# Background sums redistributed over a decoder trunk's stages, and the first feed-forward's SiLUs issued behind the following weight split

## The chip, the cores and the metric

The kernel runs on one core of a Trainium2 chip. The metric is the device time of one execution in microseconds (us); the time before is the median of three runs, 1927.47 us (1927.08 to 1927.84). Everything here is about one program of about 12,000 instructions on five engines: PE (matrix products), ACT (activation functions and copies), DVE (elementwise work and sums), POOL (small odd work) and SP (issues the weights' DMA transfers). PEld in the profile is the loading of the stationary operand of a matrix product.

## The reference

Two layers over 256 tokens of width 2048. Layer 0 mixes by causal pooling, layer 1 by latent attention; each is followed by a SwiGLU feed-forward network (FFN) of width 5632. Each sub-layer's norm is shifted and scaled, and its residual gated, by vectors made from one conditioning vector `c`.

```python
sc = silu(c)
for i in range(2):
    shift_m, scale_m, gate_m, shift_f, scale_f, gate_f = split(sc @ mod_w[i] + mod_b[i], 6)
    if i == 1:
        kv_shift, kv_scale = split(sc @ kv_mod_w + kv_mod_b, 2)
        h_kv = rmsnorm(x, kv_in_norm) * (1 + kv_scale) + kv_shift
        ckv = rmsnorm(h_kv @ w_dkv, kv_norm)
        k_nope, v, k_rope = ckv @ w_uk, ckv @ w_uv, rope(h_kv @ w_kr)
    h = rmsnorm(x, norm_mix[i]) * (1 + scale_m) + shift_m
    if i == 0:
        y = pool_mixer(h)
    else:
        cq = rmsnorm(h @ w_dq, q_norm)
        y = attention(rope(cq @ w_uq), k_nope, k_rope, v) @ w_o
    x = x + gate_m * y
    h = rmsnorm(x, norm_ffn[i]) * (1 + scale_f) + shift_f
    x = x + gate_f * ((silu(h @ w_gate) * (h @ w_up)) @ w_down)
return rmsnorm(x, final_norm)
```

## The kernel before

**Weight units.** Weights arrive as units of 512 x 512 numbers (one 1 MB transfer into a `raw` tile, six of which rotate). Each unit is split into two halves of higher and lower bits: the upper half is a copy on ACT (line 374, tile `hl`), the lower a subtraction on DVE (line 376, another `hl`). Six `hl` tiles rotate, so three units can be ahead of PE. A product of a unit with 256 tokens is 24 matmuls of 128x512 (line 398: upper weights with both halves of the activations, then lower weights) or, for keys and queries, which come out transposed, 48 of 128x256 (line 1296). Two tokens' blocks ("tok") go to two PSUM banks (`ps`); in the last unit of a sum the first bank's twelve matmuls stand ahead of the second's, so that it can be read earlier.

**Background sums.** The products of `silu(c)` with the modulation weights that are not needed at once are made on DVE: `Part.unit` loads 128 rows of the transposed weights (1 MB, a `raw` tile too, line 210) and multiplies and sums them along the row in one instruction (line 211). 168 such sums stand in a list. `split` calls `tick` before each weight unit; `tick` adds a rate to a credit and issues a sum for each whole credit, until a goal (a number left in the list) is met. `plan(left, units)` and `release(left, units)` set the goal and the rate = (sums left in the list - goal)/units. From `hold` (near the end of an FFN) to `release` no sum is issued. After the sixteenth sum of a gate, DVE adds the bias (line 300) and `spread` turns the column on PE (line 292) and sends it through DRAM to all partitions.

**Stages.** In the order of time: the pooling layer; the first FFN (eleven chunks of 512, in the steps of `FFN_STEPS`: p projects a chunk to gate and up, t turns the chunk for the down product, d is a down product of a group); a handover whose order is written by hand (`then_attention`); keys and values in four groups, each one `w_uk` unit (line 1296) and one `w_uv` unit (line 398); between them the modulated input of the queries (`hidden_q`: transposes on PE, line 540, then lines 558 and 559 on ACT and 560 on DVE), then four `w_dq` units for the queries' latent, whose norm is lines 1246 to 1249 (ACT squares and sums, DVE, a power on POOL at line 1248, DVE scales) and which is turned (line 540) and split (lines 1259 on ACT, 1261 on DVE); the heads' weights `w_uq` (split on lines 1458 and 1459; first product on line 1370); attention by head pairs; the output product; the second FFN.

**What sets the order.** Outside the stretches written by hand, a scheduler of the recording layer sets each engine's order when the program is built, by priorities and its own estimate of when operands are there; `issue_after` makes it put an instruction behind a named one. Each engine then works strictly in that order, and waits at the first instruction whose operand isn't there. Functions put into `pending` are called in `flush` at the next split and issued behind that split's two instructions. SiLUs of a chunk (line 802) are in the program right behind the gate's last product; each reads one bank. Then come the up product's units, and DVE multiplies both (line 806); the result is turned on PE (line 729) and split (lines 732 and 733).

**The numbers.** When the first FFN is planned, 144 sums are left, of which 48 belong to the second FFN. With `MIX_LATE` 14, 82 are spread over 93 units; 92 units tick before `hold`, which makes 81 sums. `release` then finds 63 and goes down to 48 + `MIX_DQ` = 54: 9 sums over `MLA_UNITS` = 4 units (2, 2, 2 and 3). The `w_uv` unit of the third group has none. `plan(n_all, DQ_UNITS)` gives the last 6 to the next units at 1.2 each; as the program is built, one stands beside each of the six units that follow (four `w_dq`, `w_uk` and `w_uv` of the fourth group).

Of the kernel before, what the change touches and what calls it, by code (L numbers as in the profile page):

```python
# [13 lines left out]
AF = mybir.ActivationFunctionType  # L14
# [46 lines left out]
BEGUN = 6  # L61
ASIDE = 5

FFN0_UNITS, MLA_UNITS, DQ_UNITS, WO_UNITS, FFN1_UNITS = 93, 4, 5, 8, 60

KNOWN = (1, 3, 5, 7, 9, 10, 11, 12)


LATE, MIX_LATE, MIX_DQ = 3, 14, 6

V_C, V_NM, V_NF, V_KVIN, V_KVN, V_QN, V_PS, V_B, V_KB, V_END = 0, 16, 48, 80, 96, 100, 104, 120, 312, 344

# [21 lines left out]
def tile_trunk(ctx: ExitStack, tc: tile.TileContext, a: dict, out: bass.AP):  # L94
    nc = tc.nc
    sync, act, dve, pe, pool = nc.sync, nc.scalar, nc.vector, nc.tensor, nc.gpsimd
# [20 lines left out]
    def t2k(shape, dt=F32):  # L117
        return work.tile(shape, dt, tag="t2k", bufs=7, name=nm("t2k"))
# [152 lines left out]
    pending = []  # L271
# [307 lines left out]
    def stream_aside(l):  # L579
        if l == 0:  # L580
            return
        aside[l] = dram.tile([P, NT, D], F32, name=nm("aside"))
        with tc.issue_after(w_load[0].ins):
            sync.dma_start(aside[l], x)
# [129 lines left out]
    def ffn(l, hT, gate_name, begun, then):  # L714
# [3 lines left out]
        def project(c, which):  # L718
            if c in begun:
                begun[c][which].block(ND - 1, hT[ND - 1])  # L720
                return begun[c][which].result()
            return proj(ffn_weights(l)[which][:, c], hT)
# [67 lines left out]
        def project_chunk(c):  # L790
            if c == ASIDE:
                stream_aside(l)
            if c == NF - 1:
                end = StreamEnd(l)
                stream_end.append(end)
                for n, wait in enumerate(KNOWN):
                    pending.append((wait, lambda n=n: end.known(n // NT, n % NT, gates[gate_name])))
            gb = project(c, GATE)
            nat[c] = []
            for tok in range(NT):  # L800
                sg = t2k([P, CH])
                act.activation(sg, gb[tok], AF.Silu)  # L802
                nat[c].append(sg)
            ub = project(c, UP)
            for tok in range(NT):
                dve.tensor_tensor(out=nat[c][tok], in0=ub[tok], in1=nat[c][tok], op=ALU.mult)  # L806

        for step in FFN_STEPS:
            {"p": project_chunk, "t": transposed, "d": down}[step[0]](int(step[1:]))
# [848 lines left out]
```

## Time and profile before

| | |
|---|---|
| median of three runs | 1927.47 us (1927.08 to 1927.84) |
| the profiled execution | 1927.86 us, of which the span from first to last instruction is 1926.1 us |
| mean granted TensorE clock | 0.987 of full speed |
| ACT busy | 830.0 us (43%) |
| bytes read from HBM | 567.76 MB, 298 GB/s over the span |
| PE busy in 950 to 985 us (keys and values) | 29.28 of 35.00 us |

The page of the profile gives busy time for each engine, then the span in 40 slices, then the chain of work that ended last, followed back from the end. A busy engine is not a bound by itself; what bounds is read from the waits of the engine that is on the chain, and from what released them. A row of the timeline has the start in us, the length, the engine, line and operation, what is written and read, the shape, how many equal instructions were put together, and in brackets the engine's idle time before it and who ended it.

### The profile page before, as it was taken

How to read it: one execution, taken by the hardware profiler on the slowest of the kernel's cores; microseconds unless marked ns; L12 is line 12 of the kernel's file. 1: busy time of each engine (PE TensorE's matmuls, PEld its weight loads, DVE VectorE, ACT ScalarE, POOL GpSimd, SP SyncE). 2: the span in 40 equal slices, each digit the busy share in tenths (PEclk: the TensorE clock that was granted, in tenths of full speed). 3: DMA queues.
4: the chain of work that ended last, by engine and by line, in shares of the span. 5: the costliest groups of instructions: out<-in, count | busy, mean ns of one | idle time of the engine just before them, and what ended most of it. 6: DMA issues, size and time to landing. Idle time of an engine off the chain costs nothing.

```text
span 1926.1 us, 21857 instructions
## 1 busy us (share of the span) xinstructions
PE 1863.2 (97%) x8797; PEld 1508.1 (78%) x8797; DVE 1412.7 (73%) x1394; ACT 830.0 (43%) x904; POOL 20.9 (1%) x30
## 2 busy tenths in 40 slices
PE   7689999999999999999989999999999999999998
PEld 3256888888888888887879888888888888888887
DVE  2148799999788778789897886889786566645566
ACT  3125643443433334344665745634444433433343
POOL 0000000000000000000100000000000000000000
PEclk9889999999999999999999999999999999999999
DMA  9999998889989899896595394988776666665551
GB/s 398 393 418 417 370 358 340 320 312 357 364 346 380 328 353 353 351 379 260 210 379 199 123 363 180 399 333 319 268 286 240 233 243 245 243 225 209 218 197 44
DMA packets 81655, 575.51 MB, mean 299 GB/s; under 512 B 8929, under 2 KB 9361, under 8 KB 13201
## 3 DMA queue, kind: packets, MB, share of 16 engines
q1 hardware_dynamic: 81026, 570.94, 77.1%
q0 software_dynamic: 432, 3.15, 0.4%
q8 instruction: 69, 1.13, 0.2%
q14 instruction: 32, 0.26, 0.0%
q10 hardware_dynamic: 96, 0.02, 0.0%
HBM read 567.76 MB, written 6.32 MB: 298 GB/s over the span
## 4 chain that ended last, share of the span: by engine, by line
PE 90%; DMA 4%; DVE 3%; ACT 1%; issue 1%; SPq 0%; POOL 0%; POOLq 0%; DVEq 0%; ACTq 0%
PE ps L398 75%; DMA raw<-in_mod_w_dram 3%; PE ps L256 2%; PE ps L1296 2%; PE ps L977 2%; PE ps L407 2%; DVE hl L376 1%; PE ps L729 1%; DVE raw L211 1%; PE ps L1475 1%; ACT hl L374 1%; PE ps L1208 1%; DMA raw<-in_mod_block_dram 0%; DMA raw<-in_w_uk_dram 0%; PE ps L196 0%
## 5 line engine op out<-in xcount | busy, mean ns | idle before, releaser
L398 PE MATMUL ps<-hl,act 128*128 128x512 f32 x6672 | 1526.9, 390 | 8.6 <-ACT hl L374 6.5
L398 PEld LDWEIGHTS ps<-hl,act 128*128 128x128 f32 x6672 | 1251.7, 188 | 272.1 <-ACT hl L374 8.4
L376 DVE TENSOR_TENSOR hl<-raw,hl 128x2048 fp32r<-128x2048 f32 x286 | 653.8, 2289 | 247.9 <-ACT hl L374 247.3
L374 ACT ACTIVATE hl<-raw 128x2048 fp32r<-128x2048 f32 x286 | 546.6, 1918 | 604.1 <-PE ps L398 433.8
L211 DVE SCALAR_TENSOR_TENSOR raw<-raw,s_row 128x2048 f32<-128x2048 f32 x168 | 383.0, 2285 | 2.0 <-DMA raw<-in_mod_wt_dram 2.0
L256 PE MATMUL ps<-raw,s_strip 128*32 128x512 f32 x392 | 63.2, 739 | 36.5 <-DMA raw<-in_mod_w_dram 36.2
L698 DVE TENSOR_TENSOR act<-ps,act 128x512 f32<-128x512 f32 x96 | 64.5, 685 | 17.2 <-PE ps L398 17.2
L256 PEld LDWEIGHTS ps<-raw,s_strip 128*32 128x32 f32 x392 | 9.4, 119 | 69.3 <-DMA raw<-in_mod_w_dram 45.9
L1296 PE MATMUL ps<-act,hl 128*128 128x256 f32 x384 | 49.5, 286 | 1.1 <-DVE hl L376 1.1
L1296 PEld LDWEIGHTS ps<-act,hl 128*128 128x128 f32 x384 | 48.1, 194 | 1.8 <-DVE hl L376 1.3
L407 PE MATMUL ps<-hl,act 128*128 128x512 f32 x192 | 47.0, 398 | 1.1 <-DVE hl L520 0.9
L802 ACT ACTIVATE t2k<-ps 128x512 f32<-128x512 f32 x24 | 14.2, 590 | 71.7 <-PE ps L398 71.7
L407 PEld LDWEIGHTS ps<-hl,act 128*128 128x128 f32 x192 | 35.2, 188 | 10.6 <-ACT act L490 1.5
L742 DVE TENSOR_TENSOR x<-ps,x 128x512 f32<-128x512 f32 x32 | 21.8, 689 | 28.8 <-PE ps L398 28.8
L732 ACT ACTIVATE act<-ps 128x512 fp32r<-128x512 f32 x44 | 23.3, 594 | 43.2 <-PE ps L729 30.5
L263 DVE COPY t2k<-ps 128x256 f32<-128x256 f32 x4 | 1.7, 425 | 52.8 <-ACT t2k L262 52.8
L427 ACT ACTIVATE junk<-x 128x512 bf16<-128x512 f32 x23 | 14.5, 630 | 54.5 <-DVE x L612 37.3
L806 DVE TENSOR_TENSOR t2k<-ps,t2k 128x512 f32<-128x512 f32 x24 | 16.6, 690 | 28.7 <-PE ps L398 28.7
L520 DVE TENSOR_TENSOR hl<-raw,hl 128x2048 fp32r<-128x2048 f32 (+2 forms) x16 | 31.8, 1987 | 5.7 <-ACT hl L517 5.7
L977 PEld LDWEIGHTS ps<-act,act 128*128 128x128 f32 x128 | 25.0, 202 | 11.7 <-issue 8.4
L977 PE MATMUL ps<-act,act 128*128 128x256 f32 x128 | 32.4, 406 | 0.0
L696 ACT ACTIVATE act<-ps 128x512 f32<-128x512 f32 x32 | 19.1, 597 | 28.7 <-PE ps L398 28.6
(221 smaller groups left out, 927.4 us busy)
## 6 DMA issues: line engine op xcount, KB each, us to landing
raw<-in_mod_wt_dram SPq DMA_DIRECT2D x136, 1024.0 KB, 6.7
raw<-in_ffn_gate_dram SPq DMA_DIRECT2D x88, 1024.0 KB, 6.3
raw<-in_ffn_up_dram SPq DMA_DIRECT2D x88, 1024.0 KB, 5.9
raw<-in_ffn_down_dram SPq DMA_DIRECT2D x88, 1024.0 KB, 4.9
raw<-in_mod_w_dram SPq DMA_DIRECT2D x48, 1024.0 KB, 11.7
raw<-in_kv_mod_wt_dram SPq DMA_DIRECT2D x32, 1024.0 KB, 7.6
raw<-in_w_o_dram SPq DMA_DIRECT2D x16, 1024.0 KB, 7.2
raw<-in_mod_block_dram SPq DMA_DIRECT2D x8, 1024.0 KB, 12.4
```

The lines of the kernel that those rows point to most:

```text
L211: dve.scalar_tensor_tensor(out=r, in0=r, scalar=1.0, in1=s_row, op0=ALU.mult, op1=ALU.mult, accum_out=self.sums[:, self.n:self.n + 1])
L256: pe.matmul(self.bank[m * STRIP:(m + 1) * STRIP, :], lhsT=weights(k), rhs=r[:, k, i, :], start=first, stop=last)
L374: hi_ins = act.activation(hi, r, AF.Copy)
L376: lo_ins = dve.tensor_tensor(out=lo, in0=r, in1=hi.bitcast(F32), op=ALU.subtract)
L398: pe.matmul(banks[tok], lhsT=t_[:, i, k, tok * P:(tok + 1) * P], rhs=w[:, k, :], start=first and n < len(part), stop=last and n >= len(ord ...
L407: pe.matmul(bank, lhsT=t_[:, i, k, tok * P:(tok + 1) * P], rhs=w[:, k, :], start=first and n == 0, stop=last and n == len(order) - 1)
L520: dve.tensor_tensor(out=w[2][:, ks], in0=w[0][:, ks], in1=w[1][:, ks].bitcast(F32), op=ALU.subtract)
L698: dve.tensor_tensor(out=part, in0=banks[tok], in1=part, op=ALU.add)
L732: act.activation(m[:, 0, :, ts_], v, AF.Copy)
L742: dve.tensor_tensor(out=sums, in0=bank, in1=sums, op=ALU.add)
L977: pe.matmul(mixed[g][:, n % 2, :], lhsT=wp[g][:, k, ns], rhs=pool_all[g // 2][:, g % 2, k, :], start=k == 0, stop=k == KL - 1)
L1296: pe.matmul(pt[:, h, :], lhsT=w(h0 + h, k), rhs=t_[:, i, k, :], start=n == 0, stop=n == 3 * KL - 1)
```

## The change

Three numbers change, and one line of `ffn`.

```diff
--- before.py
+++ after.py
@@ -61,12 +61,12 @@
 BEGUN = 6
 ASIDE = 5
 
-FFN0_UNITS, MLA_UNITS, DQ_UNITS, WO_UNITS, FFN1_UNITS = 93, 4, 5, 8, 60
+FFN0_UNITS, MLA_UNITS, DQ_UNITS, WO_UNITS, FFN1_UNITS = 93, 4, 6, 8, 60
 
 KNOWN = (1, 3, 5, 7, 9, 10, 11, 12)
 
 
-LATE, MIX_LATE, MIX_DQ = 3, 14, 6
+LATE, MIX_LATE, MIX_DQ = 3, 12, 7
 
 V_C, V_NM, V_NF, V_KVIN, V_KVN, V_QN, V_PS, V_B, V_KB, V_END = 0, 16, 48, 80, 96, 100, 104, 120, 312, 344
 
@@ -799,7 +799,7 @@
             nat[c] = []
             for tok in range(NT):
                 sg = t2k([P, CH])
-                act.activation(sg, gb[tok], AF.Silu)
+                pending.append((0, lambda sg=sg, bank=gb[tok]: act.activation(sg, bank, AF.Silu)))
                 nat[c].append(sg)
             ub = project(c, UP)
             for tok in range(NT):
```

`MIX_LATE` 12 instead of 14 leaves two sums fewer for after the first FFN: 84 over 93 units, 83 by `hold`. `release` finds 61 and goes down to 48 + 7 = 55: 6 sums over four units (1, 2, 1 and 2). `plan(n_all, DQ_UNITS)` spreads the last 7 over 6 units, 7/6 each (five units with one, the last with two). From the first key unit to the heads there are 13 sums instead of 15. The SiLUs go into `pending` with no wait, and so are issued behind both instructions of the next split, which is that of the first unit of the up product. All 22 SiLU pairs of both FFNs go this way.

The built programs have the same instructions on each engine; their order differs. The first place is ACT in the first FFN, seventh to eighth projected chunk; `hl` of line 374 is the upper half of a weight unit, `t2k` of line 802 the SiLU's result, `ps` its bank. Before:

```order
L374 ACTIVATE hl_4029<-raw_4024 128x2048
L374 ACTIVATE hl_4062<-raw_4057 128x2048
L802 ACTIVATE t2k_4090<-ps_3954 128x512
L374 ACTIVATE hl_4101<-raw_4096 128x2048
L802 ACTIVATE t2k_4092<-ps_3955 128x512
L374 ACTIVATE hl_4134<-raw_4129 128x2048
```

Now:

```order
L374 ACTIVATE hl_4032<-raw_4027 128x2048
L374 ACTIVATE hl_4065<-raw_4060 128x2048
L374 ACTIVATE hl_4102<-raw_4097 128x2048
L802 ACTIVATE t2k_4093<-ps_3957 128x512
L802 ACTIVATE t2k_4094<-ps_3958 128x512
L374 ACTIVATE hl_4137<-raw_4132 128x2048
```

The split that stood between the two SiLUs stands ahead of both. The same happens in the three other chunks of the first FFN that had this order; the chunks that had both SiLUs behind the split keep it, and on PE's side the second FFN's waits are on the same instructions as before.

The second place is ACT in the third key group. `hl_6518<-raw_6516` before and `hl_6515<-raw_6513` now are the split of the same `w_uv` unit, the one that follows the transposes of the queries' input on PE; lines 558 and 559 modulate that input; lines 1288 and 1297 copy finished values and keys out of PSUM. Before:

```order
L1288 ACTIVATE act_6310<-ps_6376 128x512
L1297 ACTIVATE act_6415<-ps_6431 128x512
L1297 ACTIVATE act_6415<-ps_6457 128x512
L558 ACTIVATE t2k_6498<-ps_6483,cols 128x256
L558 ACTIVATE t2k_6502<-ps_6483,cols 128x256
L559 ACTIVATE act_6497<-t2k_6498 128x256
L559 ACTIVATE act_6497<-t2k_6502 128x256
L558 ACTIVATE t2k_6506<-ps_6488,cols 128x256
L558 ACTIVATE t2k_6510<-ps_6488,cols 128x256
L559 ACTIVATE act_6497<-t2k_6506 128x256
L559 ACTIVATE act_6497<-t2k_6510 128x256
L374 ACTIVATE hl_6518<-raw_6516 128x2048
```

Now:

```order
L1288 ACTIVATE act_6313<-ps_6378 128x512
L374 ACTIVATE hl_6515<-raw_6513 128x2048
L1288 ACTIVATE act_6313<-ps_6379 128x512
L1297 ACTIVATE act_6415<-ps_6428 128x512
L374 ACTIVATE hl_6601<-raw_6596 128x2048
L1297 ACTIVATE act_6415<-ps_6454 128x512
L558 ACTIVATE t2k_6495<-ps_6480,cols 128x256
```

The `w_uv` split, and that of the first `w_dq` unit (`hl_6601`), stood behind the eight modulations and stand ahead of them now, the first of them two copies earlier still.

The third place is where the queries' latent is normed and the attention's gate is finished, on DVE and PE. `raw` on line 211 is a sum, lines 1247 and 1249 the norm of the two token blocks, line 376 here the lower half of the fourth group's `w_uv` unit, line 300 the gate's bias. DVE before:

```order
L1247 TENSOR_SCALAR sm_6750<-sm_6749 128x1
L211 SCALAR_TENSOR_TENSOR raw_6769,sums_5661<-raw_6769,s_row 128x2048
L1249 TENSOR_SCALAR t2k_6752<-ps_6580,sm_6751 128x512
L1247 TENSOR_SCALAR sm_6759<-sm_6758 128x1
L1249 TENSOR_SCALAR t2k_6761<-ps_6581,sm_6760 128x512
L376 TENSOR_TENSOR hl_6856<-raw_6849,hl_6855 128x2048
L211 SCALAR_TENSOR_TENSOR raw_6851,sums_5661<-raw_6851,s_row 128x2048
L1261 SCALAR_TENSOR_TENSOR act_6838<-ps_6828,vcol,act_6838 128x256 x2
L1459 TENSOR_TENSOR hl_6890<-raw_6887,hl_6889 128x1536
L1261 SCALAR_TENSOR_TENSOR act_6838<-ps_6833,vcol,act_6838 128x256 x2
L1459 TENSOR_TENSOR hl_6948<-raw_6945,hl_6947 128x1536
L300 TENSOR_TENSOR cols<-sums_5661,vcol 128x16
```

DVE now:

```order
L211 SCALAR_TENSOR_TENSOR raw_6766,sums_5587<-raw_6766,s_row 128x2048
L1247 TENSOR_SCALAR sm_6747<-sm_6746 128x1
L1249 TENSOR_SCALAR t2k_6749<-ps_6577,sm_6748 128x512
L376 TENSOR_TENSOR hl_6856<-raw_6846,hl_6855 128x2048
L1247 TENSOR_SCALAR sm_6756<-sm_6755 128x1
L211 SCALAR_TENSOR_TENSOR raw_6848,sums_5587<-raw_6848,s_row 128x2048
L1249 TENSOR_SCALAR t2k_6758<-ps_6578,sm_6757 128x512
L211 SCALAR_TENSOR_TENSOR raw_6851,sums_5587<-raw_6851,s_row 128x2048
L1261 SCALAR_TENSOR_TENSOR act_6835<-ps_6825,vcol,act_6835 128x256 x2
L300 TENSOR_TENSOR cols<-sums_5587,vcol 128x16
L1459 TENSOR_TENSOR hl_6890<-raw_6887,hl_6889 128x1536
```

One sum stands ahead of the first norm and one between the two halves of the second; the subtraction of the `w_uv` unit, which stood behind both norms, stands between them; line 300 stands ahead of both subtractions of line 1459 instead of behind the two. On PE, the transposes of the normed latent (line 540) before:

```order
L1296 MATMUL ps_6802<-act_6199,hl_6772 128x256 x4
L540 MATMUL ps_6828<-con,t2k_6752 128x128
L540 MATMUL ps_6828<-con,t2k_6761 128x128
L540 MATMUL ps_6828<-con,t2k_6752 128x128
L540 MATMUL ps_6828<-con,t2k_6761 128x128
L540 MATMUL ps_6833<-con,t2k_6752 128x128
L540 MATMUL ps_6833<-con,t2k_6761 128x128
L540 MATMUL ps_6833<-con,t2k_6752 128x128
L540 MATMUL ps_6833<-con,t2k_6761 128x128
L398 MATMUL ps_6847<-hl_6855,act_6199 128x512 x8
```

Now:

```order
L1296 MATMUL ps_6799<-act_6205,hl_6769 128x256 x4
L540 MATMUL ps_6825<-con,t2k_6749 128x128
L540 MATMUL ps_6830<-con,t2k_6749 128x128
L398 MATMUL ps_6844<-hl_6855,act_6205 128x512 x5
L540 MATMUL ps_6825<-con,t2k_6758 128x128
L540 MATMUL ps_6825<-con,t2k_6749 128x128
L540 MATMUL ps_6825<-con,t2k_6758 128x128
L540 MATMUL ps_6830<-con,t2k_6758 128x128
L540 MATMUL ps_6830<-con,t2k_6749 128x128
L540 MATMUL ps_6830<-con,t2k_6758 128x128
L398 MATMUL ps_6844<-hl_6855,act_6205 128x512 x3
```

Five matmuls of the `w_uv` unit stand between the second and third transpose, so the second token block's norm is needed that much later.

## The prediction

> **What bounds the kernel now.** First the page: busy times, the chain of work that ended last, and the costliest group (busy us, mean ns of one, idle us before it).
>
> ```profile
> PE 1863.2 (97%) x8797; PEld 1508.1 (78%) x8797; DVE 1412.7 (73%) x1394; ACT 830.0 (43%) x904; POOL 20.9 (1%) x30
> PE 90%; DMA 4%; DVE 3%; ACT 1%; issue 1%; SPq 0%; POOL 0%; POOLq 0%; DVEq 0%; ACTq 0%
> ...
> L398 PE MATMUL ps<-hl,act 128*128 128x512 f32 x6672 | 1526.9, 390 | 8.6 <-ACT hl L374 6.5
> ```
>
> PE is busy 97% of the span and makes 90% of the chain, and the change removes no matmul. So the time can change only by what PE waits, and by the clock that it is granted behind a wait. Second, therefore, PE's waits behind 170 us (ahead of it nothing is moved): what PE waited for, us in total, times, longest.
>
> ```profile
> PE ps L398 <- ACT hl L374: 6.5, 5, 4.7
> PE ps L292 <- DVE cols L300: 2.0, 1, 2.0
> PE ps L482 <- DVE t2k L476: 1.7, 1, 1.7
> PE ps L398 <- DVE hl L376: 1.1, 2, 0.6
> PE ps L1296 <- DVE hl L376: 1.1, 1, 1.1
> ```
>
> Five waits are for the upper split on ACT: one of 4.7 us and four of (6.5 - 4.65)/4 = 0.46 each. The gate's bias (L300) costs 2.0 once, a lower split (L376) 1.1 once. L482 is in the handover, which keeps its order; the two of 0.6 lie beside lines 611 and 612 at the end of the first FFN, where the new order moves a wait from one product to the next, which I cost at nothing, between -0.6 and +0.6.
>
> Third, the timeline of all engines at one of the four small waits.
>
> ```profile
> 632.53 0.60 ACT L802 ACTIVATE t2k<-ps 128x512 f32<-128x512 f32 x1 [14.18 <-PE ps L398]
> 633.03 1.91 ACT L374 ACTIVATE hl<-raw 128x2048 fp32r<-128x2048 f32 x1
> ...
> 634.99 2.36 PE L398 MATMUL ps<-hl,act 128*128 128x512 f32 x9 [0.45 <-ACT hl L374]
> ```
>
> ACT had been idle for 14.18 us with nothing that it could do but the split, and did the SiLU first; the split then ended 0.45 us too late for PE. Fourth, PE and ACT at the larger waits.
>
> ```profile
> 963.70 1.92 ACT L374 ACTIVATE hl<-raw 128x2048 fp32r<-128x2048 f32 x1 [2.56 <-DMA raw<-in_w_uk_dram]
> ...
> 973.10 0.60 ACT L1297 ACTIVATE act<-ps 128x512 f32<-128x512 f32 x1 [1.80 <-PE ps L1296]
> ...
> 976.62 3.72 ACT L374 ACTIVATE hl<-raw 128x2048 fp32r<-128x2048 f32 x2
> ```
>
> ```profile
> 968.00 5.06 PE L1296 MATMUL ps<-act,hl 128*128 128x256 f32 x40 [1.07 <-DVE hl L376]
> 972.91 1.03 PE L540 MATMUL ps<-con,t2k 128*128 128x128 f32 x8
> 978.59 7.36 PE L398 MATMUL ps<-hl,act 128*128 128x512 f32 x24 [4.65 <-ACT hl L374]
> ...
> 986.59 22.02 PE L398 MATMUL ps<-hl,act 128*128 128x512 f32 x96
> 1008.44 5.92 PE L1296 MATMUL ps<-act,hl 128*128 128x256 f32 x48
> 1014.20 1.04 PE L540 MATMUL ps<-con,t2k 128*128 128x128 f32 x8
> 1014.99 5.73 PE L398 MATMUL ps<-hl,act 128*128 128x512 f32 x24
> 1022.69 0.28 PE L292 MATMUL ps<-con,cols 128*16 128x128 f32 x1 [1.97 <-DVE cols L300]
> ```
>
> Two things follow a wait. A matmul alone takes 0.39 us (the mean of 390 ns above), but in a row (22.02 - 0.39)/95 = 0.228, so each wait costs 0.16 more than its gap. And the clock: the granted clock (PEclk, the figure ahead of DMA's share) in two stretches of L398, and in three of all engines.
>
> ```profile
> 978.59:982.09 3.50, 3.50 (x8) 2.76 (x9) 0.52 1.02 424
> 988.00:991.50 3.50, 3.50 (x17) 2.88 (x17) 1.00 0.99 403
> ...
> 906.42:908.42 2.00, 2.00 (x11) 1.53 (x11) 0.70 (x2) 1.68 (x5) 0.00 (x0) 1.00 0.10 41
> ...
> 1023.00:1025.00 2.00, 2.00 (x12) 2.00 (x11) 1.51 (x1) 0.27 (x1) 0.00 (x0) 0.52 1.00 326
> 1022.72:1028.48 5.76, 5.76 (x36) 5.76 (x37) 3.45 (x5) 0.27 (x2) 0.61 (x1) 0.70 0.97 358
> 1028.48:1032.80 4.32, 4.32 (x38) 4.32 (x37) 1.69 (x4) 0.60 (x1) 0.00 (x0) 1.00 0.73 283
> ```
>
> Behind the 4.65 us PE ran at about half clock: 24 matmuls in 7.36 us, where the same 24 at 1014.99 took 5.73, a loss of 1.63. Behind the 1.97 us too (0.52): 5.76 us for the head work that took 4.32 the next time, a loss of 1.44. Behind the handover's 1.7 us the clock stayed 1.00.
>
> **The change, part by part.** *The SiLUs.* The four splits that stood between two SiLUs now stand ahead of both, so four gaps go: 4 x (0.46 + 0.16) = 2.5 us. What is late next: the SiLUs end up to 1.9 us later, but the multiplication that reads them waits for the up product, four units' matmuls away. The other 18 pairs already stood behind the split and cost nothing either way.
>
> *Order at the FFN's end.* In the new order the transposes (L729) of the last chunk stand alone behind its up product; before, those of the chunk ahead came between.
>
> ```profile
> 857.84 1.91 PE L729 MATMUL ps<-con,t2k 128*128 128x128 f32 x16
> ...
> 858.04 0.69 DVE L806 TENSOR_TENSOR t2k<-ps,t2k 128x512 f32<-128x512 f32 x1 [1.21 <-PE ps L398]
> ```
>
> The second bank's multiplication ends at 858.73. Sixteen transposes take (1.91 - 0.28)/15 = 0.109 each, 0.28 being one alone (as at 1022.69); with only the first bank's four ahead, the fifth is due at 857.84 + 0.44 = 858.28. PE will wait 0.5 us; between nothing (if the first bank's own wait swallows it) and 1.
>
> *Two more sums in the first FFN.* A sum is 2.26 us of DVE (31.6/14, below). DVE's fullest 50 us of that FFN:
>
> ```profile
> 370.00:420.00 50.00, 50.00 (x234) 41.65 (x233) 48.21 (x47) 22.34 (x19) 0.00 (x0) 1.00 0.86 322
> ```
>
> DVE has 1.79 us free there, the DMA share is 0.86, and PE never waits. At 84/93 instead of 82/93 a sum per unit, 50 us (nine units) get 0.2 sums or 0.4 us more. Their two loads move with them, between those of the units in SP's queue, in transfers that are not full. Hidden by DVE's free time; I take zero, and a place where the cover is gone is the slower rival.
>
> *Keys.* The `w_uv` split that PE waited 4.65 us for stood behind two copies and eight modulations (973.10 to 976.62); it now stands ahead of the last copies and needs only its weights. Its lower half, and the lower half at 968.00, are on DVE, which decides from here:
>
> ```profile
> 951.23:1013.23 62.00, 56.28 (x312) 49.02 (x311) 57.81 (x62) 38.79 (x60) 3.01 (x2) 0.97 0.96 371
> ```
>
> ```profile
> L211 DVE SCALAR_TENSOR_TENSOR raw<-raw,s_row 128x2048 f32<-128x2048 f32 x14 | 31.6, 2286 | 0.0
> L376 DVE TENSOR_TENSOR hl<-raw,hl 128x2048 fp32r<-128x2048 f32 x9 | 20.6, 2291 | 3.0 <-ACT hl L374 2.7
> ...
> L1249 DVE TENSOR_SCALAR t2k<-ps,sm 128x512 f32<-128x512 f32 x2 | 1.5, 752 | 1.2 <-POOL sm L1248 1.2
> ```
>
> From the first sum to the second norm's end DVE works 57.81 of 62.00 us. Before the uk unit's lower half five sums stood where now three do, and before `w_uv`'s nine where now six do: 3 x 2.26 = 6.8 us earlier against 4.65 + 1.07 needed. Both waits go, and with them two restarts and the slow clock: 1.07 + 4.65 + 0.32 + 1.63 = 7.7 us.
>
> *What is late next* is the norm of the queries' latent.
>
> ```profile
> 1008.21 2.29 DVE L211 SCALAR_TENSOR_TENSOR raw<-raw,s_row 128x2048 f32<-128x2048 f32 x1
> 1008.44 2.46 POOL L1248 TENSOR_TENSOR sm<-sm,mhalf 128x1 f32<-128x1 f32 x1 [69.69 <-DVE sm L1247]
> ...
> 1011.90 0.55 POOL L1248 TENSOR_TENSOR sm<-sm,mhalf 128x1 f32<-128x1 f32 x1 [0.99 <-DVE sm L1247]
> ...
> 1017.55 0.88 DVE L1261 SCALAR_TENSOR_TENSOR act<-ps,vcol,act 128x256 fp32r<-128x256 f32 x2
> ...
> 1022.46 0.17 DVE L300 TENSOR_TENSOR cols<-sums,vcol 128x16 f32<-128x16 f32 x1
> ```
>
> The power on POOL takes 0.55 us, but 2.46 beside a sum, which it waits out. Now a sum stands between the second L1247 and L1249, so that this one is the slow one. [...]
>
> DVE's work up to the second norm: 57.81, less two sums (4.52), plus one lower split that now stands ahead (2.29) = 55.58. Idle time: at least the 1.2 of the L1249 row, at most the 4.19 of before; I take 2.2, since the row's 2.7 for ACT splits shrinks where they come earlier. The norm ends at 951.23 + 55.58 + 2.2 = 1009.0 (1008.0 to 1011.0). PE comes to the transposes at 1014.20 - 7.67 = 1006.5, and does two of them and five matmuls first (0.22 + 5 x 0.228), so needs it at 1007.9. A new wait of 1.1 us, between 0.1 and 3.1, and 0.16 for the restart. Behind the waiting transpose on PE stand the rest of `w_uv` and all heads; nothing of them can go around it.
>
> *The gate's bias.* L300 waited behind two subtractions of line 1459 and the last sum. Now, behind the second norm (1009.0): a sum 2.26, two L1261 (0.88), L300 0.17: ready at 1012.3. PE needs it after its wait and the nineteen matmuls left, about 1014. So the 1.97 goes with its restart and slow clock: 1.97 + 0.16 + 1.44 = 3.6 us. The first subtraction of line 1459 ends near 1014.2, 0.1 late.
>
> *Sum.* FFN: -2.5 + 0.5 = -2.0. Keys: -7.7 - 3.6 + 1.1 + 0.16 + 0.1 = -9.9. Together -11.9, of the profiled 1927.86 us (span 1926.1 and 1.8 around it), which is 0.4 above the median: 1916.0, and from the median **1915.6 us**.
>
> **Rivals.** *DVE stays late.* If DVE keeps all its idle time, the second norm costs 3.1 us, and a wait over 1.97 brings the half clock (1.6): 3.6 above the forecast, 1919.2. For it: 57.81 of 62 busy. Against: what it waited for comes earlier.
>
> *Loads set the pace.* The same 62 us have a DMA share of 0.96, and ACT waited 2.56 us for `w_uk`'s weights. If so, the stretch shrinks only by the two units of 1 MB not loaded: 371 GB/s makes 2.8 us each, 5.6 instead of 9.9 gained: 1919.9. Against: the sums' loads stand ahead of the units', and three are gone ahead of `w_uv`.
>
> *The clock.* If the half clock at 1023 has another cause than the 1.97 us wait, its 1.44 stays: 1917.0. The handover's 1.7 us, with the clock at 1.00, speaks for it, the 0.52 right behind the wait against. [...]
>
> *Slower.* Sums are conserved: two more in the first FFN, and all later ones there in another phase to the splits. Where a lower split's lead is under 2.26 us, PE waits up to 2.2 and pays half clock, 1.6: 3.8 each. Three such places give 1927.0, five 1934.6; from four on it is slower than before. Against: 1.79 us free in the fullest stretch, and of the waits above only two at most are L376's in that FFN. That the change doesn't do what it says can be seen for the SiLUs: only four pairs move; 2.5 is all they can give.
>
> **How the numbers follow.** Forecast 0.59 (1913.0 to 1918.0, by the norm's wait from 0.1 to 3.1, L729 and the handover's end). DVE late 0.14; loads 0.09; clock 0.08; slower mechanism with two or three places 0.06, with more 0.04. The range 1913.0 to 1921.5 leaves out the last two. A difference of 0.2% (3.9 us) is about what a measurement of this kernel can tell from none: faster 0.90, same 0.06, slower 0.04.
>
> **What would show it.** In the new profile L398's waits on L374 should be gone, L1296's on L376 and L292's on L300 too; L540 should wait 0.1 to 3.1 us for L1249; PE's clock in the keys should read 1.00; POOL should show the 2.46 at the second norm. Wrong would be: waits of L398 on L376 between 170 and 850 us, a clock of 0.5 at the first head, or an ACT split in the keys that waits for a DMA while PE is idle.

## The result and the profile after

| | before | after |
|---|---|---|
| median of five runs each, same chip | 1927.08 us | 1913.61 us |
| lowest and highest | 1925.44 to 1927.84 | 1912.56 to 1914.34 |
| span of the profiled execution | 1926.1 us | 1912.4 us |

The ratio is 0.9932 (95% interval 0.9917 to 0.9946): 13.5 us less by the medians, where 11.9 had been forecast. Two timed executions of the experiments below, of 2691.55 and 3802.14 us, are far slower than all others of their kernels and are left out of the medians. The page of the kernel after, busy times and chain:

```profile
PE 1860.8 (97%) x8797; PEld 1506.5 (79%) x8797; DVE 1412.2 (74%) x1394; ACT 830.9 (43%) x904; POOL 20.7 (1%) x30
PE 93%; DMA 4%; DVE 2%; issue 1%; ACT 0%; SPq 0%; POOL 0%; POOLq 0%; DVEq 0%; ACTq 0%
```

The work of every engine is what it was; PE's share of the chain rose from 90 to 93%, and ACT's fell from 1 to 0. PE's waits behind 170 us (what it waited for, us in total, times, longest):

```profile
PE ps L398 <- DVE hl L376: 2.2, 3, 1.1
...
PE ps L482 <- DVE t2k L476: 0.5, 1, 0.5
...
PE ps L729 <- DVE t2k L806: 0.3, 1, 0.3
```

All five waits for ACT's splits (6.5 us), that for the gate's bias (2.0) and L1296's (1.1) are gone. New is L729's 0.3, and L398's waits for lower splits at the end of the first FFN grew from 1.1 to 2.2 us, while L482's in the handover behind it shrank from 1.7 to 0.5. PE in the keys:

```profile
963.64 5.92 PE L1296 MATMUL ps<-act,hl 128*128 128x256 f32 x48
969.39 1.03 PE L540 MATMUL ps<-con,t2k 128*128 128x128 f32 x8
970.18 5.74 PE L398 MATMUL ps<-hl,act 128*128 128x512 f32 x24
...
1004.16 0.38 PE L540 MATMUL ps<-con,t2k 128*128 128x128 f32 x2
1004.30 1.40 PE L398 MATMUL ps<-hl,act 128*128 128x512 f32 x5
1005.53 0.82 PE L540 MATMUL ps<-con,t2k 128*128 128x128 f32 x6
1006.11 4.60 PE L398 MATMUL ps<-hl,act 128*128 128x512 f32 x19
1010.54 0.27 PE L292 MATMUL ps<-con,cols 128*16 128x128 f32 x1
```

No row has a bracket: PE never stops from the third group to the heads. The `w_uv` product takes 5.74 us instead of 7.36 behind a wait of 4.65. Set beside the rows of before, this says where the time went, in one execution of each. The first sum moved from 951.23 to 949.06: 2.2 us came from the first FFN and the handover. The transposes of the normed latent moved from 1014.20 to 1004.16, so 7.9 us more came from the keys. L292 moved from 1022.69 to 1010.54, 2.1 more, the gate's wait and its restart. Behind L292 the granted clock is now 1.00 (1010.54 to 1014.54), so the 1.44 of slow clock is gone too. Together these are 13.6, against 13.7 between the spans.

DVE and, in a second view, POOL at the second norm of the kernel after:

```profile
999.01 0.75 DVE L1249 TENSOR_SCALAR t2k<-ps,sm 128x512 f32<-128x512 f32 x1 [0.73 <-POOL sm L1248]
...
1001.93 2.29 DVE L211 SCALAR_TENSOR_TENSOR raw<-raw,s_row 128x2048 f32<-128x2048 f32 x1
1004.66 0.75 DVE L1249 TENSOR_SCALAR t2k<-ps,sm 128x512 f32<-128x512 f32 x1 [0.44 <-POOL sm L1248]
...
1008.33 0.16 DVE L300 TENSOR_TENSOR cols<-sums,vcol 128x16 f32<-128x16 f32 x1
```

```profile
998.42 0.55 POOL L1248 TENSOR_TENSOR sm<-sm,mhalf 128x1 f32<-128x1 f32 x1 [61.83 <-DVE sm L1247]
1002.16 2.46 POOL L1248 TENSOR_TENSOR sm<-sm,mhalf 128x1 f32<-128x1 f32 x1 [3.19 <-DVE sm L1247]
```

The slow power on POOL moved to the second norm, as the order said. The norm ends at 1004.66 + 0.75 = 1005.41, and PE's third transpose, which reads it, starts at 1005.53: 0.12 us to spare.

### The profile page after: what moved, and what is told of

Same layout as the page of the kernel before. It is cut to its first block, busy times and chain, and to the rows that moved or that the text cites. A ratio compares the mean times of both kernels' runs of the same rounds, so it can differ in the third digit from the quotient of the medians.

```text
span 1912.4 us, 21871 instructions
## 1 busy us (share of the span) xinstructions
PE 1860.8 (97%) x8797; PEld 1506.5 (79%) x8797; DVE 1412.2 (74%) x1394; ACT 830.9 (43%) x904; POOL 20.7 (1%) x30
## 3 DMA queue, kind: packets, MB, share of 16 engines
q0 software_dynamic: 432, 3.15, 0.4%
## 4 chain that ended last, share of the span: by engine, by line
PE 93%; DMA 4%; DVE 2%; issue 1%; ACT 0%; SPq 0%; POOL 0%; POOLq 0%; DVEq 0%; ACTq 0%
PE ps L398 78%; DMA raw<-in_mod_w_dram 3%; PE ps L1296 2%; PE ps L256 2%; PE ps L977 2%; PE ps L407 2%; PE ps L729 1%; PE ps L1475 1%; DVE hl L376 1%; PE ps L1208 1%; DMA raw<-in_mod_block_dram 0%; PE ps L196 0%; PE ps L540 0%; PE ps L1425 0%; PE ps L1385 0%
## 5 line engine op out<-in xcount | busy, mean ns | idle before, releaser
L398 PE MATMUL ps<-hl,act 128*128 128x512 f32 x6672 | 1525.5, 390 | 3.1 <-DVE hl L376 2.2
L398 PEld LDWEIGHTS ps<-hl,act 128*128 128x128 f32 x6672 | 1251.8, 188 | 263.9 <-DVE hl L376 3.4
L376 DVE TENSOR_TENSOR hl<-raw,hl 128x2048 fp32r<-128x2048 f32 x286 | 653.6, 2288 | 240.7 <-ACT hl L374 240.5
L1296 PE MATMUL ps<-act,hl 128*128 128x256 f32 x384 | 48.6, 284 | 0.0
L407 PE MATMUL ps<-hl,act 128*128 128x512 f32 x192 | 46.9, 398 | 1.1 <-DVE hl L520 0.9
L1296 PEld LDWEIGHTS ps<-act,hl 128*128 128x128 f32 x384 | 47.4, 192 | 0.5 <-ACT act L1259 0.2
L407 PEld LDWEIGHTS ps<-hl,act 128*128 128x128 f32 x192 | 35.2, 188 | 10.5 <-ACT act L490 1.5
```

The lines of the kernel that those rows point to most:

```text
L376: lo_ins = dve.tensor_tensor(out=lo, in0=r, in1=hi.bitcast(F32), op=ALU.subtract)
L398: pe.matmul(banks[tok], lhsT=t_[:, i, k, tok * P:(tok + 1) * P], rhs=w[:, k, :], start=first and n < len(part), stop=last and n >= len(ord ...
L407: pe.matmul(bank, lhsT=t_[:, i, k, tok * P:(tok + 1) * P], rhs=w[:, k, :], start=first and n == 0, stop=last and n == len(order) - 1)
L1296: pe.matmul(pt[:, h, :], lhsT=w(h0 + h, k), rhs=t_[:, i, k, :], start=n == 0, stop=n == 3 * KL - 1)
```

## The experiments

All were timed beside the kernel before on the same chip; a ratio is that of the run to it. Expectations stand as they were written before each run.

**The SiLU line alone** (edit on the kernel before):

```diff
-                act.activation(sg, gb[tok], AF.Silu)
+                pending.append((0, lambda sg=sg, bank=gb[tok]: act.activation(sg, bank, AF.Silu)))
```

> Only the SiLU line of the change; the three numbers as before. My theory: ACT's four late splits in the first FFN go, 4 x (0.46 + 0.16) = 2.5 us, and the keys keep all their waits (1.07, 4.65 and 1.97 us): 1924.7 us, between 1924.4 and 1925.3. Rival (ACT, idle for 14 us at these places, is no limit and the waits come back elsewhere): 1927.

Measured: 1924.22 us, ratio 0.9984 (0.9975 to 0.9992), 3.3 us less than the kernel before beside it. PE's waits in this run:

```profile
PE ps L398 <- ACT hl L374: 4.7, 1, 4.7
PE ps L292 <- DVE cols L300: 2.0, 1, 2.0
PE ps L482 <- DVE t2k L476: 1.8, 1, 1.8
```

Of five waits for ACT's split the one of 4.7 us in the keys is left; the four of 0.45 are gone and nothing took their place. The interval is 1.5 to 4.8 us, so it holds the 2.5 of the waits, and rules the rival out; the median lies 0.2 below the range that I gave. The keys did not keep all their waits in the profiled execution: L1296 waited 0.45 us instead of 1.07. What that wait hangs on is taken up with the keys below.

**The three numbers alone** (edit on the kernel before):

```diff
-FFN0_UNITS, MLA_UNITS, DQ_UNITS, WO_UNITS, FFN1_UNITS = 93, 4, 5, 8, 60
+FFN0_UNITS, MLA_UNITS, DQ_UNITS, WO_UNITS, FFN1_UNITS = 93, 4, 6, 8, 60
-LATE, MIX_LATE, MIX_DQ = 3, 14, 6
+LATE, MIX_LATE, MIX_DQ = 3, 12, 7
```

> Only the three numbers; the SiLUs in program order as before. My theory: all waits of PE in the keys go (11.2 us with restarts and slow clock), the four waits of 0.45 us in the first FFN stay: 1915.9 us, between 1915 and 1917. The two parts add up: this gain and that of the SiLU line alone make the whole within 1 us. Rival (the two extra sums in the first FFN delay splits there, and only together with the SiLU line is that hidden): more than four waits of L398 before 850 us, 1918 or more.

Measured: 1916.23 us, ratio 0.9941 (0.9929 to 0.9953), 11.3 us less. The two parts give 3.3 + 11.3 = 14.6, 1.1 more than the whole, just over the 1 us that I had allowed and within their intervals. PE's waits:

```profile
PE ps L398 <- DVE hl L376: 2.2, 3, 1.2
PE ps L398 <- ACT hl L374: 1.1, 3, 0.5
```

Three small waits for ACT's split, not four: the moved sums shift the first FFN's order a little too. The keys' waits are gone without the SiLU line, and L376's larger waits at the FFN's end are there without it, so both belong to the numbers.

**Only MIX_LATE** (edit on the change):

```diff
-FFN0_UNITS, MLA_UNITS, DQ_UNITS, WO_UNITS, FFN1_UNITS = 93, 4, 6, 8, 60
+FFN0_UNITS, MLA_UNITS, DQ_UNITS, WO_UNITS, FFN1_UNITS = 93, 4, 5, 8, 60
-LATE, MIX_LATE, MIX_DQ = 3, 12, 7
+LATE, MIX_LATE, MIX_DQ = 3, 12, 6
```

> The whole change with only MIX_DQ and DQ_UNITS put back (6 and 5): 13 sums after the first FFN as in the change, but seven instead of six ahead of the third group's value unit, and the gate's bias (L300) behind the subtractions of line 1459 again. My theory: the keys' two waits (1.07, 4.65) go or stay under 0.5 together; L300 is ready about 2 us after PE wants it, and the clock falls again behind that wait: 2.2 + 0.16 + 1.44 above the change, 1917.4 us, L292 waits 1.5 to 3 us. Rival (only the two sums that left the keys matter, not where the rest stand): 1913.6, L292 does not wait.

Measured: 1915.63 us, ratio 0.994 (0.9927 to 0.9953), some 2 us above the change and 1.8 below what I expected. PE in this run:

```profile
1010.63 0.28 PE L292 MATMUL ps<-con,cols 128*16 128x128 f32 x1 [1.99 <-DVE cols L300]
```

The two keys' waits are gone with seven sums ahead of `w_uv`'s split as with six, and the gate's bias is late again by 1.99 us, as expected. So the two sums that left the keys end the keys' waits, and the numbers of the queries' units decide whether the gate's bias is in time. But the clock did not fall behind this wait in the profiled execution (1.00 from 1010.66 to 1016.66), which is taken up again below. The missing 1.44 us of slow clock would account for most of the 1.8; this isn't shown, since only one of the five executions has a timeline, and that one (1914.32 us) also came to its first matmul of line 398 at 167.7 us, 2.0 earlier than the change did.

**MIX_LATE 14, MIX_DQ 9** (edit on the change):

```diff
-LATE, MIX_LATE, MIX_DQ = 3, 12, 7
+LATE, MIX_LATE, MIX_DQ = 3, 14, 9
```

> The whole change, but MIX_LATE 14 and MIX_DQ 9: six sums ahead of the third group's value unit as in the change, but 15 after the first FFN as before, the two more behind it. My theory: DVE paces the stretch up to the gate. The two waits of the keys are gone as in the change, but L300 stands behind two sums and a subtraction more and is 5 us later than PE wants it; with the restart and half clock behind it 6 to 7 us above the change: 1920 us (1917.5 to 1921.5). Rival (ACT's order in the third group is all that matters): 1913.6 to 1915, no wait over 1 us behind 1000 us.

Measured: 1922.79 us, ratio 0.997 (0.9958 to 0.9982). That is 9 us above the change, and above the range given. PE's timeline in this run:

```profile
1002.27 6.45 PE L1296 MATMUL ps<-act,hl 128*128 128x256 f32 x40 [1.76 <-DVE sm L1247]
...
1018.01 0.28 PE L292 MATMUL ps<-con,cols 128*16 128x128 f32 x1 [3.15 <-DVE cols L300]
```

DVE is the pace, and the rival falls: with the same six sums ahead of `w_uv`, two more behind it make PE wait twice. The first wait I had not foreseen. The lower half of the fourth group's `w_uk` stands behind two sums and the first norm there, and ends at 1002.21. Behind both the clock fell: behind the first the stretches of 2 us have a clock of 0.50 and 0.71, which loses (0.50 + 0.29) x 2 = 1.6 us, behind the second 0.77, 0.50 and 0.88, which loses 1.7. With 1.76 + 3.15 and two restarts these are 8.5 us.

**MIX_LATE 10, MIX_DQ 6, and MIX_LATE 2, MIX_DQ 2** (edits on the change):

```diff
-LATE, MIX_LATE, MIX_DQ = 3, 12, 7
+LATE, MIX_LATE, MIX_DQ = 3, 10, 6
```

> The whole change with MIX_LATE 10, MIX_DQ 6: two sums more in the first FFN (85), 11 instead of 13 behind it. My theory: PE has no wait left between the first key unit and the heads, so there is nothing to gain: 1913.6 us, 1912.5 to 1915. Rival (DVE's load still sets that stretch, each sum taken from it gains its 2.2 us): 1909 to 1911.5.

```diff
-LATE, MIX_LATE, MIX_DQ = 3, 12, 7
+LATE, MIX_LATE, MIX_DQ = 3, 2, 2
```

> The whole change with MIX_LATE 2, MIX_DQ 2: some 92 sums in the first FFN instead of 83, two or so behind it. My theory: the nine sums more are 20 us of DVE over 92 units (500 us) in which DVE had some 5 of 50 us free, so they hide: 1913.6 us, 1912.5 to 1916, at most three new waits of L398 on L376. Rival (the slower mechanism of the prediction: lower splits lose their lead, up to 3.8 us at each place): five places or more, 1920 and above.

Measured: 1912.78 us (ratio 0.9923, 0.9911 to 0.9936) and 1912.43 us (0.9922, 0.991 to 0.9934). Both are like the change (the second is 0.07 below the range given): DVE's load behind the FFN no longer costs anything, and nine more sums in the FFN cost nothing there. At the FFN's end both have fewer waits than the change: L398 waits 0.82 for ACT's split and 1.00 for a lower one, and L482 not at all. The stretch of 500 us of the first FFN in the change and then in the run with MIX_LATE 2 (busy us of PE, PEld, DVE, ACT, POOL, then clock, DMA share, GB/s):

```profile
370.00:870.00 500.00, 499.65 (x2250) 414.19 (x2249) 428.88 (x345) 195.28 (x141) 0.70 (x1) 1.00 0.91 358
```

```profile
370.00:870.00 500.00, 499.65 (x2249) 414.10 (x2248) 448.88 (x365) 196.60 (x143) 0.70 (x1) 1.00 0.94 377
```

DVE has 20.0 us more to do, PE is busy for the same 499.65: the lead of the lower splits holds with DVE at 90%.

**The hold earlier** (edits on the change; the second has `- 2 * (l == 0)` and 89 units):

```diff
-                if last and j == ND - 2:
+                if last and j == ND - 2 - (l == 0):
-FFN0_UNITS, MLA_UNITS, DQ_UNITS, WO_UNITS, FFN1_UNITS = 93, 4, 6, 8, 60
+FFN0_UNITS, MLA_UNITS, DQ_UNITS, WO_UNITS, FFN1_UNITS = 91, 4, 6, 8, 60
```

> The whole change, with the hold at the end of the first FFN two units earlier and the same 83 sums spread over 91 units. My theory: the waits of L398 on L376 in the FFN's last units (0.56, 0.50 and 1.10 us in the change) come from the last two sums, which stand ahead of line 611 and the splits there; 0.50 and at least half of 1.10 go: 1912.3 us, 1911.3 to 1913.3. Rival (the additions of lines 604 to 612 alone make the splits late): 1913.6, the three waits stay at 2 us together.

> As the run before, with the hold four units earlier and 89 units. My theory: all three waits but the one behind line 611's own wait for PE go: 1912 us, 1911 to 1913. Rival: 1913.6.

Measured: 1910.04 us (ratio 0.9908, 0.9893 to 0.9923) and 1910.0 us (0.991, 0.9897 to 0.9924), both below their ranges. More went than I expected: all three waits on L376 and L482's too. What they came from, in the change on DVE and then on PE:

```profile
879.35 2.28 DVE L211 SCALAR_TENSOR_TENSOR raw<-raw,s_row 128x2048 f32<-128x2048 f32 x1
881.56 1.28 DVE L611 TENSOR_TENSOR x<-ps,gate 128x512 f32<-128x512 f32 x2
882.76 1.28 DVE L612 TENSOR_TENSOR x<-x,act 128x512 f32<-128x512 f32 x2
...
883.96 4.49 DVE L376 TENSOR_TENSOR hl<-raw,hl 128x2048 fp32r<-128x2048 f32 x2
```

```profile
886.30 7.56 PE L398 MATMUL ps<-hl,act 128*128 128x512 f32 x32 [1.10 <-DVE hl L376]
893.69 10.13 PE L407 MATMUL ps<-hl,act 128*128 128x512 f32 x44
904.31 0.66 PE L482 MATMUL ps<-con,t2k 128*128 128x128 f32 x4 [0.48 <-DVE t2k L476]
```

The last sum stands ahead of lines 611 and 612, and those ahead of two lower splits: no idle time on DVE in all of it. With the hold earlier DVE waits for PE there, which the next row, from the run with the hold four units earlier, shows:

```profile
895.32 0.69 DVE L611 TENSOR_TENSOR x<-ps,gate 128x512 f32<-128x512 f32 x1 [1.52 <-PE ps L407]
```

**The change and this version once more**, side by side:

> The change once more, beside the next run on the same chip: 1913.6 us.

> The change with the hold four units earlier, beside the change on the same chip: 1910.0 us, 3.6 us less than the change, of which 2.2 are the three waits on L376, 0.5 the one at L482, and 0.6 four restarts.

Measured: the change 1914.2 us (ratio 0.9933, 0.992 to 0.9947), the hold four units earlier 1910.11 us (0.9912, 0.9898 to 0.9925). It beats both kernels, the change by 4.1 us, 0.5 more than expected; the waits and restarts listed are 3.3 of it.

**The clock behind the same wait.** Two programs were profiled once more, unchanged; the second ran on another chip than the first time. "Phase" in the second text is the moment in the execution at which the wait falls.

> The kernel before once more, for the clock behind the same wait. Theory A (the wait's length decides): L292 waits 1.97 us again and the granted clock of the 2 us behind it is again near 0.5 to 0.6. [...]

> The run with MIX_LATE alone once more: there a wait of 1.99 us at L292 was followed by the full clock. Theory A (something of this program, not the phase, keeps the clock up): 1.00 again, time 1914 to 1914.8. Theory B (phase): in this execution, with even chance, a stretch of half clock within 4 us behind the wait, and the time 1 to 1.6 us longer than with the full clock.

Measured: 1926.8 and 1917.71 us. L292 waited 1.96 and 1.99 us. The stretches of 2 us right behind the wait (clock ahead of DMA share), with MIX_LATE alone, first execution:

```profile
1010.66:1012.66 2.00, 2.00 (x18) 2.00 (x19) 1.95 (x2) 0.27 (x1) 0.00 (x0) 1.00 0.91 277
1012.66:1014.66 2.00, 2.00 (x19) 2.00 (x18) 1.50 (x4) 0.00 (x0) 0.00 (x0) 1.00 0.97 371
```

The same program, second execution:

```profile
1012.57:1014.57 2.00, 2.00 (x12) 2.00 (x13) 1.76 (x1) 0.27 (x1) 0.00 (x0) 0.61 1.00 335
1014.57:1016.57 2.00, 2.00 (x12) 2.00 (x12) 1.35 (x4) 0.00 (x0) 0.00 (x0) 0.54 1.02 379
1016.57:1018.57 2.00, 2.00 (x20) 2.00 (x19) 0.35 (x1) 0.00 (x0) 0.61 (x1) 1.00 0.98 381
```

The kernel before, once more:

```profile
1021.59:1023.59 2.00, 2.00 (x11) 2.00 (x12) 1.76 (x1) 0.28 (x2) 0.00 (x0) 0.55 0.92 295
1023.59:1025.59 2.00, 2.00 (x13) 2.00 (x13) 1.19 (x3) 0.00 (x0) 0.00 (x0) 0.59 0.99 372
```

One program, one wait of 1.99 us, and once a clock of 1.00 behind it, once of 0.61 and 0.54; that theory A can't give, neither by the wait's length nor by something of the program. It isn't the chip alone either: on the chip where this program kept the full clock, the run of the SiLU line lost 1.7 us behind a wait of 1.96 (clock 0.86, 0.50 and 0.79 in the three stretches of 2 us). That the moment of the wait decides (theory B) agrees with both outcomes and isn't shown: no run sets that moment. The second execution took 3.4 us more than the first, not 1 to 1.6: 1.8 of that was there when PE came to L482 (904.03 against 902.24), ahead of the keys, and the 1.7 of slow clock is about the rest. The kernel before showed nearly the first profile's clocks again (0.55 and 0.59 beside 0.59 and 0.56), so this execution alone told nothing against A.

## Why the prediction was right, and where it was not

The time, the sign and the main mechanism held: 1913.6 us lies in the range, and close to its lower end. Of the waits named, those for ACT's splits, for a lower half in the keys (L1296's) and for the gate's bias went; the new wait of 1.1 us at the second norm did not come. By the prediction's own steps:

**SiLUs (-2.5).** Right, by the run of that line alone: the four waits of 0.45 go and nothing is late behind them. **L729 (+0.5).** Right in size (0.35 and a restart), but it belongs to the numbers: the wait is in the run of the numbers alone and not in that of the SiLU line alone.

**The FFN's end (0, within 0.6).** Right in sum, but not in its parts. L376's waits grew by 1.1 us, and L482's shrank by 1.3, which the prediction had taken for fixed since the handover's order is. A fixed order doesn't fix a wait: from its last sum on DVE idled only 1.5 us (for ACT and POOL in the norm), the same in both kernels, so its own queue set when L476 came (905.87, then 903.76: 2.1 earlier). PE, held up more by L376, came to L407 only 0.9 earlier (894.54, then 893.69) and so waited less at L482. The runs with the hold earlier showed what was behind both: sums issued up to the last units.

**Two more sums in the FFN (0).** Right, and by far: even nine more cost nothing there. The rival that was to make the kernel slower needed lower splits with no lead left, and there is no wait of L398 on L376 ahead of the FFN's end even with DVE busy 448.88 of 500 us.

**Keys (-7.7).** Right in size: 7.9 by the transposes' start. Of L1296's 1.07 the prediction said that DVE decides. The traces say more. DVE in the kernel before, first execution:

```profile
956.11 2.29 DVE L376 TENSOR_TENSOR hl<-raw,hl 128x2048 fp32r<-128x2048 f32 x1 [0.38 <-ACT hl L374]
...
965.66 2.29 DVE L376 TENSOR_TENSOR hl<-raw,hl 128x2048 fp32r<-128x2048 f32 x1 [0.62 <-ACT hl L374]
```

DVE stood idle twice for ACT's splits, and ACT had stood idle 0.84 and 2.56 us for these two units' weights. In the second execution of the kernel before, DVE waits for neither split, and L1296 does not wait; in the run of the SiLU line it is 0.33 us of such idle time and a wait of 0.45. So this 1.07 came from late loads in that one execution. The 4.65 at `w_uv` is 4.65 in all three.

**The second norm (+1.1 and restart).** This is the term that was mis-sized. DVE's work was nearly as forecast, the idle time not:

```profile
949.06:1005.41 56.35, 56.35 (x327) 49.74 (x325) 55.10 (x59) 40.70 (x64) 3.01 (x2) 1.00 0.98 379
```

From the first sum to the norm's end DVE worked 55.10 us (forecast 55.58) and idled 1.25 (forecast 2.2, lower bound 1.2): the 0.73 and 0.44 for POOL and next to nothing else. I had kept 1 us for ACT's splits. Of before's 2.7 us of such idle time none was left: 0.38 and 0.62 were the late loads just named, and the 1.72 ahead of one subtraction (at 988.42) is gone too. That this is because upper splits now stand further ahead fits the new order, but no run separates it. The norm ended 56.35 us behind the first sum instead of 57.8, 0.12 us before PE needed it. So the wait is not there, but only just: the run with 15 sums behind the FFN shows what a sum or two too many cost. **L1370 (+0.1)** went with it.

**The gate (-3.6).** The 1.97 and its restart are right. The 1.44 of slow clock was a fact of the execution profiled, and is not one of every execution with such a wait. The rival of the clock, that the half clock had another cause, is not borne out: in the profile of the change, where L292 doesn't wait, the clock behind it is 1.00 (1010.54 to 1016.54). What spoke for it, that a wait of about 2 us need not bring a slow clock, is right: 1.99 us, and 1.00 behind it, with MIX_LATE alone. How often it does in the timed runs is open.

**Loads.** ACT's timeline of the kernel after at the third group's `w_uv`:

```profile
963.76 1.92 ACT L374 ACTIVATE hl<-raw 128x2048 fp32r<-128x2048 f32 x1 [2.04 <-DMA raw<-in_w_uv_dram]
```

ACT still waited for weights there, with the DMA share at 0.98 in the row above, but the split was done 4.5 us before PE's product of 970.18: the rival that loads set the pace falls, for PE in the change.

Sum: the forecast of -11.9 lacks 1.3 us for the norm and 0.1 for L1370; that makes -13.3, and 13.5 was measured. That they agree to 0.2 us is partly luck: the 1.07 and the 1.44 differ from one execution to the next, and the interval of the measured gain is 10.4 to 16.0 us.

## What to carry to other kernels

Background work on an engine that also feeds the bound engine costs nothing until an instruction in its queue is late, and then it costs the wait, the restart and perhaps a slow clock at once (at `w_uv` 4.65 us, an estimated 0.16 and 1.63); so place it by where that queue has a lead (here a long FFN, which took nine more sums for nothing), and keep it out of stretches where the queue has none (the keys, and the FFN's last units: issuing the same sums two units earlier gained some 3.5 us). When bounding what becomes late next, take the engine's work from before, but not its idle time: if that was a wait for something which the change moves earlier, it goes as well. A wait's price read from one execution holds a part that differs in the next (L1296's 1.07 us; 1.44 of slow clock behind L292); profile a kernel twice before counting on it.

## What the runs showed of the hardware

The clock behind a short wait of PE is not set by the wait's length alone. Behind L292's wait of 1.96 to 1.99 us it fell in four executions (twice in the kernel before, in the run of the SiLU line, in the second of MIX_LATE alone) and stayed at 1.00 in one; behind L482's of 1.7 to 1.8 it stayed at 1.00 in four of four (twice in the kernel before, in the runs of the SiLU line and of MIX_LATE 14). Where it fell at L292, the loss was the same: in the second execution of MIX_LATE alone (1 - 0.61) x 2 + (1 - 0.54) x 2 = 1.70 us; in the kernel before once more (0.45 + 0.41) x 2 = 1.72. Behind the same wait of 4.65 us at `w_uv` it was not: 1.7 and 1.6 us in the two executions of the kernel before, and 2.8 in the run of the SiLU line, where three stretches of 2 us have a clock of 0.50, 0.50 and 0.62; no run here shows why it was longer. A slow clock also stood behind L1296's wait of 1.76 us in the run with MIX_LATE 14 (0.50 and 0.71).

The power on POOL, 128x1, took 0.55 us in the queries' norm, and 2.46 where a sum had started on DVE 0.23 us ahead of it: in the kernel before at the first norm, in the change at the second. In the run with MIX_LATE 10 a subtraction of line 1459, of 1.75 us, stood at the second norm instead, and line 1249 started 2.25 us behind line 1247; beside a sum that was 2.79, with neither 0.87 (kernel before). It went with the order and not with the instruction.
